# SwiGLU by seven products: 17 inner tiles instead of 14, in another order of products, two of them added onto banks already read; the first two tiles split from float32 copies

## The chip, the cores and the metric

The kernel runs on one core of one Trainium2 chip. The metric is the device time of one execution in microseconds. Three runs of the kernel before took 1377.49, 1380.51 and 1381.48 us, median 1380.51.

## The reference

One decoder layer on 528 columns that matter (16 meta tokens and 512 positions) and 1024 channels: a half-weighted SwiGLU, a mixer (forgetting attention and retention), and a second half-weighted SwiGLU. The change touches the two SwiGLUs alone:

```python
def rmsnorm(x, g):
    y = xf * lax.rsqrt(jnp.mean(xf * xf, axis=-1, keepdims=True) + EPS)
    return y * g

def swiglu(x, w_in, w_out):                       # w_in 1024 x 5632, w_out 2816 x 1024
    a, b = jnp.split(x @ w_in, 2, axis=-1)
    return (jax.nn.silu(a) * b) @ w_out

h = h + 0.5 * swiglu(rmsnorm(h, norm_ffn1), w_ffn1_in, w_ffn1_out)
h = h + mixed(h)                                  # attention, retention, gates, w_out
h = h + 0.5 * swiglu(rmsnorm(h, norm_ffn2), w_ffn2_in, w_ffn2_out)
return h[:, LEAD:]
```

## The kernel before

All activations lie transposed, 128 channels on the partitions and the positions in the free dimension: `h[0..7]`, 128 x 528. Each product in float32 is made of three float32r passes: a tensor is split into a high part and a low part (`split`, lines 104 to 106: ScalarE copies the high part, VectorE subtracts it), and TensorE adds high x high, high x low and low x high (`mm3`, `mm3s`, line 300).

A feed-forward (`ffn`) has 22 inner tiles of 128 channels. Inner tile j has 128 columns of the gate half `a` and 128 of the value half `b` of `w_in`, each over 8 chunks of 128 input channels; one such tile of `w_in` is 1 MB. `SEQ` writes out by hand the order of TensorE's work: `n0 n1` are the first two tiles, `aJ bJ` a plain tile in two halves (48 matmuls each in the first feed-forward, 24 in the second), `uK` sums of the normed input, `eJ lJ` a tile by seven products (`early`, `late`), and `pG` one of the 8 out-projections of tile group G. The four groups have 6, 5, 6 and 5 tiles; each `pG` can only come after its group's last tile. The second feed-forward runs the same sequence on 512 columns instead of 528.

A tile by seven products takes the 2 x 2 blocks (input channels in two halves, positions in two halves of 264 or 256 columns, outputs `a` and `b`) and makes them from seven block products instead of eight. Each block product is 12 matmuls of 264 (256) columns. It needs sums of weight blocks (`wsums`, lines 188 to 191, four VectorE operations of 128 x 512) and of input blocks (`usums`), and sums of the products. VectorE makes these last sums as the products come out of the banks: tiles `b[0]` to `b[3]` from a pool `pq` of 4 PSUM banks. In `early` (lines 403 to 417) four products go to the four banks; in `late` (from line 419) the fifth, sixth and seventh go to banks 0, 2 and 3 again.

TensorE's order is the program's order. In the rest, a scheduler places the instructions of ScalarE (ACT), VectorE (DVE), GpSimd (POOL) and SyncE (SP); each engine then runs its own in order, with semaphores between them. Weights go in pieces of up to 128 x 1024 through rings of 7 high tiles (`wh`) and 5 low ones (`wl`). For a seven-product tile SP loads the whole float32 tile (`w`, two buffers), and ACT and DVE split it and its sums. For all other pieces (kind "w") POOL issues a transfer of the high part (line 201), ACT copies its negative to `wl` (line 227), and POOL issues a second, accumulating transfer onto `wl` (line 228). `weights()` looks ahead: 6 pieces begun, 4 made ready.

At the start SP loads tile 0 of `w_in` in four parts (`w0a`, `w0b`) between the eight `h`; ACT and DVE split it and scale `h` (`gained`, lines 306 and 307). Tile 1 (`n1`) is of kind "w".

Of the kernel before, what the change touches and what calls it, by code (L numbers as in the profile page):

```python
# [25 lines left out]
S = 512  # L26
# [10 lines left out]
          e6 p0 p0 l6 p0 e7 p0 p0 l7 p0 p0 p0  # L37
          e8 l8 e9 a10 l9 b10 e11 p1 l11 p1 p1 e12 p1 l12 p1 e13 p1 l13 p1 p1
          e14 a15 l14 b15 e16 l16 e17 p2 p2 l17 p2 e18 p2 p2 l18 p2 p2 p2
          e19 l19 e20 a21 l20 b21 p3 p3 p3 p3 p3 p3 p3 p3""".split()  # L40
# [24 lines left out]
def layer(tc, order, hT, wf1i, wf1o, wf2i, wf2o, wmix, wsq, vecs, cs, rmask, rvec, cmask, outT):  # L65
# [3 lines left out]
    with ExitStack() as es:  # L69
# [65 lines left out]
        def feed_ffn(seq, w_in, w_out):  # L135
            at_, nxt = {}, [0] * len(PJ)
            for tok in seq:
# [12 lines left out]
                if c in "nae":  # L150
# [3 lines left out]
                        "e": [("A0", "S1"), ("A2", "S0")], "l": [("A1", "S2"), ("A3",)]}[c]  # L154
                pieces.extend((at_[j], x, 1024) for x in cuts)
# [12 lines left out]
        def load(n):  # L168
            while at["l"] < min(n, len(loads)):
                i = at["l"]  # L170
                src, w, kind = loads[i]
                at["l"] += 1
                if kind == "w":
                    raw[i] = src
                    continue
                if st["sp"] is None:
                    at["l"] -= 1
                    return
                raw[i] = st["sp"].tile([128, 2048], F32, name=f"w{i}", tag="wS", bufs=2)
                nc.sync.dma_start(raw[i], src)  # L180
# [12 lines left out]
        def begin(n):  # L193

            while at["c"] < min(n, len(pieces)):
# [4 lines left out]
                if i >= 2 and loads[li][2] == "w":  # L200
                    nc.gpsimd.dma_start(high[i][:, :w], loads[li][0][:, c:c + w])  # L201

        def ready(n):
            begin(n)
            while at["p"] < min(n, len(pieces)):
# [11 lines left out]
                if i < 2:  # L217
                    for x in (0, 512):
                        split(wh[:, x:x + 512], wl[:, x:x + 512], raw[li][i][:, x:x + 512])
                        gained(2 * i + x // 512, gn1, u, 0, "n1")  # L220
                elif loads[li][2] == "S":
                    for x, src in enumerate(c):
                        src = (raw, sums)[src[0] == "S"][li][:, 512 * int(src[1]):512 * int(src[1]) + 512]
                        split(wh[:, 512 * x:512 * x + 512], wl[:, 512 * x:512 * x + 512], src)
# [18 lines left out]
        w0 = [wp.tile([128, 1024], F32, name=f"w0{x}", tag="wl", bufs=5) for x in "ab"]  # L243
        raw[0] = w0
        at["l"] = 1
        for k in range(KC):
            if k < 4:
                nc.sync.dma_start(w0[k // 2][:, 512 * (k % 2):512 * (k % 2) + 512], wf1i[0][:, 512 * k:512 * k + 512])
# [26 lines left out]
        nc.gpsimd.tensor_scalar_mul(kg, kg0, -0.5)  # L275
        R = cp.tile([128, T], F32, name="R")
# [21 lines left out]
        def mm3s(out, w, x, start=True, stop=True):  # L298
            for i, (p, q) in enumerate(((w[0], x[0]), (w[0], x[1]), (w[1], x[0]))):
                nc.tensor.matmul(out, p, q, start=start and i == 0, stop=stop and i == 2)  # L300
# [61 lines left out]
        def ffn(seq, u, gain, a, pst, pq, norm, done, name):  # L362
# [5 lines left out]
            def prod(out, w, off, x, k0, ts, first, last):  # L368

                for k in range(4):  # L370
                    c = slice(off + 128 * k, off + 128 * k + 128)
                    mm3s(out, [z[:, c] for z in w], [z[k0 + k][:, ts] for z in x], first and k == 0, last and k == 3)
# [27 lines left out]
            def early(j):  # L400

                b = [pq(f"{name}q{j}_{x}")[:, :nh] for x in range(4)]
                cu = ttile(f"{name}cu{j}")[:, :2 * nh]
                d = ttile(f"{name}d{j}")[:, :nh]
                bv = ttile(f"{name}b{j}")[:, :2 * nh]
# [12 lines left out]

            def late(j, b, cu, d, bv):
                w = weights()  # L420
                prod(b[0], w, 0, u, 4, t1, True, True)
                prod(b[2], w, 512, u, 4, t2, True, True)
                prod(b[3], weights(), 0, xb, 0, x2, True, True)
                sv = ttile(f"{name}s{j}")[:, :2 * nh]
                nc.vector.tensor_tensor(sv[:, x1], b[0], R[:, t1], ALU.mult)
                nc.vector.tensor_tensor(sv[:, x2], b[2], R[:, t2], ALU.mult)
                nc.vector.tensor_tensor(bv[:, x1], bv[:, x1], b[3], ALU.add)
                nc.vector.tensor_tensor(sv[:, x1], sv[:, x1], cu[:, x1], ALU.add)
                nc.vector.tensor_tensor(sv[:, x2], sv[:, x2], d, ALU.add)
                nc.scalar.activation(sv, sv, AF.Silu)  # L430
# [51 lines left out]
        with tc.tile_pool(name="psA", bufs=1, space=PSUM, reuse_waits="tile") as pA, \  # L482
                tc.tile_pool(name="s1", bufs=1, reuse_waits="tile") as sp1:
            st["sp"] = sp1
# [28 lines left out]
        st["sp"] = None  # L513
        u = nu
# [720 lines left out]
```

## Time and profile before

| | before |
|---|---|
| median of three runs | 1380.51 us (1377.49 to 1381.48) |
| the profiled execution's own time | 1377.54 us |
| its span, first to last instruction | 1375.8 us |
| FFN1, by the timeline of TensorE | 6.1 to about 385 us |
| mixer | about 386 us to 1021 us |
| FFN2 | about 1021 us to 1373 us |
| TensorE's granted clock over the span | 0.998 of full |

All times of rows are microseconds from the span's start, unless marked ns. PE is TensorE, PEld its weight loads. A matmul's own duration overlaps with the next one's, so a tile's time is read from the start of its first matmul to the start of the next tile's first matmul. A number in brackets at a row's end is the engine's idle time just before, and what released it.

### The profile page before, as it was taken

The page shows a single profiled execution, that of the slowest core. Times are in us where ns is not written, and L with a number is a line of the kernel's source. Part 1 is how long each engine was busy: PE and PEld are TensorE (multiplying, and loading weights), DVE is VectorE, ACT ScalarE, POOL GpSimd, SP SyncE. Part 2 cuts the span into 40 slices and gives each one's busy share as a digit, 9 for nine tenths or more (in the row PEclk, how much of TensorE's full clock was granted, in tenths as well). Part 3 has the DMA queues.
Part 4 walks back from the last instruction along what each step waited for, and adds up shares of the span by engine and source line. Part 5 has one row for each costly group of instructions (what it writes and reads, how often), then busy time and mean ns, then how long its engine had stood idle before and what let it go on. Part 6 is the DMA issues. An engine that isn't in the chain of part 4 may idle for free.

```text
span 1375.8 us, 22630 instructions
## 1 busy us (share of the span) xinstructions
PE 1350.0 (98%) x8871; PEld 1229.2 (89%) x8871; DVE 815.5 (59%) x1765; ACT 658.1 (48%) x1131; POOL 319.4 (23%) x462
## 2 busy tenths in 40 slices
PE   6999999999999999999999999999999999999999
PEld 5999999999989788888889998888888889999897
DVE  4876767756456655566654665523337767677552
ACT  5533334332457777777754443553436333343331
POOL 3111111121432323333221212323421111111121
PEclk9999999999999999999999999999999999999999
DMA  9456555574996767767676667889986565565656
GB/s 308 102 145 135 134 145 150 132 158 94 250 239 157 164 144 170 167 150 174 144 184 143 136 143 152 200 211 237 254 205 123 150 133 142 148 161 151 131 126 149
DMA packets 67274, 224.92 MB, mean 163 GB/s; under 512 B 8016, under 2 KB 8400, under 8 KB 63584
## 3 DMA queue, kind: packets, MB, share of 16 engines
q0 software_dynamic: 55936, 181.59, 60.3%
q1 hardware_dynamic: 11088, 41.84, 8.6%
q8 instruction: 70, 1.15, 0.3%
q14 instruction: 36, 0.29, 0.1%
q10 hardware_dynamic: 144, 0.04, 0.0%
HBM read 215.02 MB, written 8.42 MB: 162 GB/s over the span
## 4 chain that ended last, share of the span: by engine, by line
PE 89%; ACT 4%; issue 3%; DVE 2%; DMA 1%; POOL 1%; POOLq 0%; ACTq 0%
PE fq L300 10%; PE sq L300 10%; PE fpo L290 9%; PE spo L290 9%; PE pg L290 5%; PE prv L290 3%; PE oa L290 3%; PE prg L290 3%; PE spa L290 3%; PE spb L290 3%; PE ow L290 3%; PE ob L290 3%; PE fpa L290 3%; PE fpb L290 3%; PE pq L290 3%
## 5 line engine op out<-in xcount | busy, mean ns | idle before, releaser
L227 ACT ACTIVATE wl<-wh 128x1024 fp32r<-128x1024 f32 (+2 forms) x183 | 175.5, 960 | 160.5 <-PE prg L290 23.2
L105 ACT ACTIVATE wh<-w 128x512 fp32r<-128x512 f32 x112 | 70.6, 630 | 255.9 <-PE fq L300 60.9
L106 DVE TENSOR_TENSOR wl<-w,wh 128x512 fp32r<-128x512 f32 x112 | 76.5, 683 | 14.9 <-issue 14.6
L228 POOL DMA_DIRECT2D wl<-in_wmix x65 | 57.3, 881 | 108.2 <-ACT wl L227 94.5
L201 POOL DMA_DIRECT2D wh<-in_wmix x65 | 36.4, 560 | 183.6 <-PE pv L290 32.5
L290 PE MATMUL fpo<-fgl,wh 128*128 128x272 f32 x352 | 71.4, 284 | 0.0
L290 PE MATMUL fpo<-fgh,wh 128*128 128x272 f32 x352 | 71.3, 284 | 0.0
L290 PE MATMUL fpo<-fgh,wl 128*128 128x272 f32 x352 | 71.2, 284 | 0.0
L290 PE MATMUL spo<-sgl,wh 128*128 128x512 f32 (+1 forms) x181 | 70.1, 387 | 0.0
L290 PE MATMUL spo<-sgh,wl 128*128 128x512 f32 (+1 forms) x181 | 70.1, 387 | 0.0
L290 PE MATMUL spo<-sgh,wh 128*128 128x512 f32 (+1 forms) x181 | 70.1, 387 | 0.0
L106 DVE TENSOR_TENSOR pl<-PT,ph 128x512 fp32r<-128x512 f32 (+4 forms) x80 | 33.8, 433 | 47.8 <-ACT ph L105 47.3
L1130 DVE SCALAR_TENSOR_TENSOR hh<-spo,hh 128x512 f32<-128x512 f32 (+1 forms) x33 | 22.2, 674 | 59.7 <-PE spo L290 59.7
L106 DVE TENSOR_TENSOR wl<-ws,wh 128x512 fp32r<-128x512 f32 x84 | 57.5, 684 | 0.0
L105 ACT ACTIVATE wh<-ws 128x512 fp32r<-128x512 f32 x84 | 51.9, 618 | 7.3 <-DVE ws L189 6.4
L290 PEld LDWEIGHTS fpo<-fgh,wl 128*128 128x128 f32 x352 | 54.0, 188 | 0.0
L290 PEld LDWEIGHTS fpo<-fgl,wh 128*128 128x128 f32 x352 | 53.9, 188 | 0.0
L290 PEld LDWEIGHTS fpo<-fgh,wh 128*128 128x128 f32 x352 | 53.9, 188 | 0.0
L290 PE MATMUL pg<-n2uh,wh 128*128 128x512 f32 x128 | 53.8, 421 | 0.0
L505 DVE SCALAR_TENSOR_TENSOR h<-fpo,h 128x528 f32<-128x528 f32 x32 | 22.6, 706 | 48.5 <-PE fpo L290 48.5
L807 ACT ACTIVATE P<-P,st 128x144 f32<-128x144 f32 (+1 forms) x64 | 36.6, 571 | 29.5 <-DVE st L803 28.1
L290 PE MATMUL pg<-n2uh,wl 128*128 128x512 f32 x128 | 50.6, 395 | 0.0
(951 smaller groups left out, 4610.9 us busy)
## 6 DMA issues: line engine op xcount, KB each, us to landing
wh<-in_wmix POOLq DMA_DIRECT2D x65, 512.0 KB, 4.8
wl<-in_wmix POOLq DMA_DIRECT2D x65, 512.0 KB, 7.0
w<-in_wf1i SPq DMA_DIRECT2D x14, 1024.0 KB, 5.1
w<-in_wf2i SPq DMA_DIRECT2D x14, 1024.0 KB, 5.6
wh<-in_wsq POOLq DMA_DIRECT2D x24, 512.0 KB, 5.4
wl<-in_wsq POOLq DMA_DIRECT2D x24, 512.0 KB, 7.8
wh<-in_wf2i POOLq DMA_DIRECT2D x16, 512.0 KB, 5.5
wl<-in_wf2i POOLq DMA_DIRECT2D x16, 512.0 KB, 6.7
```

The source lines that it names most:

```text
L105: nc.scalar.activation(xh, src, AF.Copy)
L106: nc.vector.tensor_tensor(xl, src, f32(xh), ALU.subtract)
L201: nc.gpsimd.dma_start(high[i][:, :w], loads[li][0][:, c:c + w])
L227: nc.scalar.activation(wl[:, :w], f32(wh[:, :w]), AF.Copy, scale=-1.0)
L228: nc.gpsimd.dma_start(wl[:, :w], raw[li][:, c:c + w], accum_op=ALU.add)
L290: nc.tensor.matmul(out, p[:, o:o + 128], q[:, a:b], start=first and k == 0 and i == 0, stop=last and k == nk - 1 and i == 2)
L300: nc.tensor.matmul(out, p, q, start=start and i == 0, stop=stop and i == 2)
L505: nc.vector.scalar_tensor_tensor(h[m][:, x:y], ps, 0.5, h[m][:, x:y], ALU.mult, ALU.add)
L807: last["exp"] = nc.scalar.activation(P[i][:, :w], P[i][:, :w], AF.Exp, scale=-1.0, bias=st[:, 2:3], accum_out=sm[:, 0:1])
L1130: nc.vector.scalar_tensor_tensor(h[m][:, x:y], ps, 0.5, h[m][:, x:y], ALU.mult, ALU.add)
```

## The change

Three things change.

1. `SEQ`: tiles 10, 15 and 21, plain before, become seven-product tiles, so 17 of 22 in each feed-forward instead of 14. The out-projections stand at other places between `e` and `l`.
2. `early` and `late` make the same seven products in another order. `early` now has five: the first to bank 0, the second to bank 1, the third to bank 2, the fourth *added onto bank 0* (`onto`, no clearing at its start), the fifth to bank 3. `late` has two, both in one bank `b` (`fr`, `sr`): the sixth, and the seventh added onto it. VectorE reads such a bank twice, before and after the second product is added: in `early` bank 0 by lines 416 and 423, in `late` by lines 435 and 437. VectorE's sums are 9 operations per tile instead of 11. The pieces of weights are cut as 1024, 512, 1024 and 1024 columns, each split by one ACT and one DVE instruction, instead of seven pairs of 512.
3. The start: tile 1's weights are loaded by SP as float32 (`load(2)`, right behind the last `h`) and split by ACT and DVE, as tile 0's are. POOL's transfers of the next four pieces' high parts wait for a small copy `there` that reads the last `h`. The pool of the float32 tiles is opened before the start for that.

The diff, cut to its core:

```diff
 SEQ = """n0 n1 a2 u0 b2 u1 a3 u2 b3 u3 a4 b4 e5 l5
-          e6 p0 p0 l6 p0 e7 p0 p0 l7 p0 p0 p0
-          e8 l8 e9 a10 l9 b10 e11 p1 l11 p1 p1 e12 p1 l12 p1 e13 p1 l13 p1 p1
-          e14 a15 l14 b15 e16 l16 e17 p2 p2 l17 p2 e18 p2 p2 l18 p2 p2 p2
-          e19 l19 e20 a21 l20 b21 p3 p3 p3 p3 p3 p3 p3 p3""".split()
+          e6 p0 l6 p0 p0 e7 p0 l7 p0 e8 p0 l8 p0 p0
+          e9 l9 e10 l10 e11 p1 l11 p1 e12 p1 l12 p1 p1 e13 p1 l13 p1 p1
+          e14 l14 e15 l15 e16 l16 e17 p2 l17 p2 p2 e18 p2 l18 p2 e19 p2 l19 p2 p2
+          e20 l20 e21 l21 p3 p3 p3 p3 p3 p3 p3 p3""".split()
...
-                        "e": [("A0", "S1"), ("A2", "S0")], "l": [("A1", "S2"), ("A3",)]}[c]
-                pieces.extend((at_[j], x, 1024) for x in cuts)
+                        "e": ["A0", "S2", "S0"], "l": ["A2"]}[c]
+                pieces.extend((at_[j], x, 512 if x == "S2" else 1024) for x in cuts)
...
-                if kind == "w":
+                if kind == "w" and i > 1:
                     raw[i] = src
                     continue
...
-                if i >= 2 and loads[li][2] == "w":
-                    nc.gpsimd.dma_start(high[i][:, :w], loads[li][0][:, c:c + w])
+                if i >= 4 and loads[li][2] == "w":
+                    with tc.issue_after(hold.ins) if i < 8 else ExitStack():
+                        nc.gpsimd.dma_start(high[i][:, :w], loads[li][0][:, c:c + w])
...
+                elif i < 4:
+                    split(wh, wl, raw[li][:, c:c + w])
                 elif loads[li][2] == "S":
-                    for x, src in enumerate(c):
-                        src = (raw, sums)[src[0] == "S"][li][:, 512 * int(src[1]):512 * int(src[1]) + 512]
-                        split(wh[:, 512 * x:512 * x + 512], wl[:, 512 * x:512 * x + 512], src)
+                    o = 512 * int(c[1])
+                    split(wh[:, :w], wl[:, :w], (raw, sums)[c[0] == "S"][li][:, o:o + w])
...
+        there = cp.tile([128, 1], F32, name="there")
+        hold = nc.gpsimd.tensor_copy(there, h[KC - 1][:, 0:1])
...
-            def prod(out, w, off, x, k0, ts, first, last):
+            def prod(out, w, off, x, k0, ts, onto=False):
                 for k in range(4):
                     c = slice(off + 128 * k, off + 128 * k + 128)
-                    mm3s(out, [z[:, c] for z in w], [z[k0 + k][:, ts] for z in x], first and k == 0, last and k == 3)
+                    mm3s(out, [z[:, c] for z in w], [z[k0 + k][:, ts] for z in x], not onto and k == 0, k == 3, onto)
...
             def early(j):
                 b = [pq(f"{name}q{j}_{x}")[:, :nh] for x in range(4)]
...
-                w = weights()
-                prod(b[0], w, 0, u, 0, t1, True, True)
-                nc.vector.tensor_tensor(cu[:, x1], b[0], R[:, t1], ALU.mult)
-                prod(b[1], w, 512, xa, 0, x2, True, True)
-                nc.vector.tensor_tensor(cu[:, x2], cu[:, x1], b[1], ALU.add)
-                w = weights()
-                prod(b[2], w, 512, xa, 0, x1, True, True)
-                nc.vector.tensor_tensor(d, cu[:, x2], b[2], ALU.add)
-                prod(b[3], w, 0, xb, 0, x1, True, True)
-                nc.vector.tensor_tensor(bv[:, x1], cu[:, x2], b[3], ALU.add)
-                nc.vector.tensor_tensor(bv[:, x2], d, b[3], ALU.add)
-                return b, cu, d, bv
+                w = weights()
+                prod(b[0], w, 0, u, 0, t1)
+                nc.vector.tensor_tensor(cu[:, x1], b[0], R[:, t1], ALU.mult)
+                prod(b[1], weights(), 0, u, 4, t2)
+                nc.vector.tensor_tensor(sv[:, x2], b[1], R[:, t2], ALU.mult)
+                v = weights()
+                prod(b[2], v, 512, xa, 0, x2)
+                nc.vector.tensor_tensor(cu[:, x2], cu[:, x1], b[2], ALU.add)
+                prod(b[0], w, 512, u, 4, t1, True)
+                nc.vector.tensor_tensor(sv[:, x1], b[0], R[:, t1], ALU.mult)
+                prod(b[3], v, 0, xa, 0, x1)
+                nc.vector.tensor_tensor(d, cu[:, x2], b[3], ALU.add)
+                nc.vector.tensor_tensor(sv[:, x2], sv[:, x2], d, ALU.add)
+                nc.scalar.activation(sv, sv, AF.Silu)
+                return cu, d, sv
 
-            def late(j, b, cu, d, bv):
-                w = weights()
-                prod(b[0], w, 0, u, 4, t1, True, True)
-                prod(b[2], w, 512, u, 4, t2, True, True)
-                prod(b[3], weights(), 0, xb, 0, x2, True, True)
-                sv = ttile(f"{name}s{j}")[:, :2 * nh]
-                nc.vector.tensor_tensor(sv[:, x1], b[0], R[:, t1], ALU.mult)
-                nc.vector.tensor_tensor(sv[:, x2], b[2], R[:, t2], ALU.mult)
-                nc.vector.tensor_tensor(bv[:, x1], bv[:, x1], b[3], ALU.add)
-                nc.vector.tensor_tensor(sv[:, x1], sv[:, x1], cu[:, x1], ALU.add)
-                nc.vector.tensor_tensor(sv[:, x2], sv[:, x2], d, ALU.add)
-                nc.scalar.activation(sv, sv, AF.Silu)
+            def late(j, cu, d, sv):
+                b = pq(f"{name}r{j}")[:, :nh]
+                bv = ttile(f"{name}b{j}")[:, :2 * nh]
+                w = weights()
+                prod(b, w, 0, xb, 0, x1)
+                nc.vector.tensor_tensor(bv[:, x2], d, b, ALU.add)
+                prod(b, w, 512, xb, 0, x2, True)
+                nc.vector.tensor_tensor(bv[:, x1], cu[:, x2], b, ALU.add)
                 nc.vector.tensor_tensor(sv, sv, bv, ALU.mult)
                 return sv
```

How the order on the engines moves, at three places. TensorE, first feed-forward, inside `late`, where the sixth product ends and the seventh begins; `fq` are the banks of `early`, `fr` the new bank of `late`, `fxbh`/`fxbl` the split input sums. Before (tile 5):

```order
L300 MATMUL fq_2_900<-n1uh_172,wh_691 128x264
L300 MATMUL fq_2_900<-n1ul_173,wh_691 128x264
L300 MATMUL fq_2_900<-n1uh_172,wl_836 128x264
L300 MATMUL fq_3_901<-fxbh_533,wh_780 128x264 [waits DVE_49]
L300 MATMUL fq_3_901<-fxbl_534,wh_780 128x264
L300 MATMUL fq_3_901<-fxbh_533,wl_906 128x264
```

After (tile 6):

```order
L306 MATMUL fr_1154<-fxbh_774,wh_987 128x264
L306 MATMUL fr_1154<-fxbl_775,wh_987 128x264
L306 MATMUL fr_1154<-fxbh_774,wl_1049 128x264
L306 MATMUL fr_1154<-fxbh_534,wh_987 128x264 [waits DVE_49]
L306 MATMUL fr_1154<-fxbl_535,wh_987 128x264
L306 MATMUL fr_1154<-fxbh_534,wl_1049 128x264
```

Before, the seventh product went to bank 3, last filled by the fourth product. Now it goes onto the bank that the sixth has just filled, and its first matmul waits for VectorE.

VectorE, first feed-forward, tile 5, from the sum `d` to the end of the tile's sums; `ws` are weight sums of a coming tile, `wl` splits of its weights, `fs` becomes silu's input, `fb` the value half. Before:

```order
L413 TENSOR_TENSOR fd_903<-fcu_902,fq_2_900 128x264 [waits DVE_49,PE_49]
L415 TENSOR_TENSOR fb_904<-fcu_902,fq_3_901 128x264 [waits PE_49]
L416 TENSOR_TENSOR fb_904<-fd_903,fq_3_901 128x264 [waits DVE_49]
L425 TENSOR_TENSOR fs_1021<-fq_0_898,R 128x264 [waits PE_49]
L428 TENSOR_TENSOR fs_1021<-fs_1021,fcu_902 128x264 [waits DVE_49]
L426 TENSOR_TENSOR fs_1021<-fq_2_900,R 128x264 [waits PE_49]
L429 TENSOR_TENSOR fs_1021<-fs_1021,fd_903 128x264 [waits DVE_49]
L427 TENSOR_TENSOR fb_904<-fb_904,fq_3_901 128x264 [waits PE_49]
L106 TENSOR_TENSOR wl_1072<-w_692,wh_1005 128x512 [waits Activation_49]
L431 TENSOR_TENSOR fs_1021<-fs_1021,fb_904 128x528 [waits DVE_49,Activation_49]
```

After:

```order
L425 TENSOR_TENSOR fd_898<-fcu_897,fq_3_896 128x264 [waits DVE_49,PE_49]
L188 TENSOR_TENSOR ws_1157<-w_1111 128x512 [waits DMAHW1_49,DVE_49]
L426 TENSOR_TENSOR fs_899<-fs_899,fd_898 128x264 [waits DVE_49]
L189 TENSOR_TENSOR ws_1157<-ws_1157,w_1111 128x512 [waits DVE_49]
L435 TENSOR_TENSOR fb_986<-fd_898,fr_985 128x264 [waits PE_49]
L190 TENSOR_TENSOR w_1111<-w_1111 128x512
L191 TENSOR_TENSOR ws_1157<-w_1111,ws_1157 128x512 [waits DVE_49]
L437 TENSOR_TENSOR fb_986<-fcu_897,fr_985 128x264 [waits PE_49]
L438 TENSOR_TENSOR fs_899<-fs_899,fb_986 128x528 [waits DVE_49,Activation_49]
```

The read of `fr` at line 435, for which TensorE's seventh product waits, stands behind two operations on weight sums of 512 columns each.

POOL at the start, from its last constant; `in_wf1i` is `w_in` of the first feed-forward. Before:

```order
L269 CAST bones<-bo_109 128x128 [waits Pool_49]
L201 DMA wh_184<-in_wf1i 128x1024
L201 DMA wh_207<-in_wf1i 128x1024
L201 DMA wh_209<-in_wf1i 128x1024
L201 DMA wh_211<-in_wf1i 128x1024
L201 DMA wh_216<-in_wf1i 128x1024
L228 DMA wl_186<-in_wf1i 128x1024 [waits Activation_49]
```

After:

```order
L273 CAST bones<-bo_113 128x128 [waits Pool_49]
L281 COPY there<-h_84 128x1 [waits DMAHW4_49]
L202 DMA wh_210<-in_wf1i 128x1024
L202 DMA wh_212<-in_wf1i 128x1024
L202 DMA wh_217<-in_wf1i 128x1024
L202 DMA wh_326<-in_wf1i 128x1024 [waits DVE_49,PE_49]
L230 DMA wl_219<-in_wf1i 128x1024 [waits Activation_49]
```

Before, the first accumulating transfer (`wl_186`) was for tile 1. Now it is for tile 2 (`wl_219`); it stands behind a load (`wh_326`) that waits for VectorE and TensorE, and all loads stand behind the copy `there` of the last `h`.

## Rows read from the trace of the kernel before

**Rows 1.** The page: busy time (share of the span) and instructions by engine.

```profile
PE 1350.0 (98%) x8871; PEld 1229.2 (89%) x8871; DVE 815.5 (59%) x1765; ACT 658.1 (48%) x1131; POOL 319.4 (23%) x462
```

**Rows 2.** Waits of TensorE: line, what for, total us, times, longest.

```profile
PE fpa L290 <- DMA wl<-in_wf1i: 6.9, 1, 6.9
...
PE k2pm L648 <- ACT k2sh L105: 2.1, 1, 2.1
```

**Rows 3.** Windows: us, each engine's busy us, granted clock, DMA share, GB/s.

```profile
26.00:32.00 6.00, 3.43 (x15) 3.43 (x16) 0.99 (x2) 1.38 (x2) 2.32 (x3) 0.50 1.08 247
...
100.00:150.00 50.00, 50.00 (x413) 50.00 (x413) 30.05 (x56) 16.21 (x27) 7.16 (x10) 1.00 0.55 135
450.00:500.00 50.00, 46.76 (x276) 39.51 (x275) 29.68 (x98) 36.76 (x78) 16.19 (x23) 1.00 0.76 168
```

**Rows 4.** Timeline of TensorE, tiles 1 and 2: start, us, line, operation.

```profile
21.02 0.41 PE L290 MATMUL fpa<-n1uh,wh 128*128 128x272 f32 x2
...
28.57 0.81 PE L290 MATMUL fpa<-n1uh,wl 128*128 128x272 f32 x2 [6.90 <-DMA wl<-in_wf1i]
...
35.77 0.60 PE L322 MATMUL fpa<-acc,onesD 128*128 128x256 f32 x2
...
42.69 0.29 PE L290 MATMUL fpa<-n1uh,wh 128*128 128x272 f32 x1
...
48.53 0.29 PE L290 MATMUL fpb<-n1uh,wh 128*128 128x272 f32 x1
```

**Rows 5.** Timeline of TensorE: first matmuls of plain and seven-product tiles, FFN1 and FFN2.

```profile
77.73 0.28 PE L300 MATMUL fq<-n1uh,wh 128*128 128x264 f32 x1
...
87.92 0.28 PE L300 MATMUL fq<-n1uh,wh 128*128 128x264 f32 x1
...
1044.13 0.40 PE L290 MATMUL spa<-n3uh,wh 128*128 128x512 f32 x1
...
1055.24 0.40 PE L290 MATMUL spa<-n3uh,wh 128*128 128x512 f32 x1
...
1077.45 0.28 PE L300 MATMUL sq<-n3uh,wh 128*128 128x256 f32 x1
...
1087.40 0.28 PE L300 MATMUL sq<-n3uh,wh 128*128 128x256 f32 x1
```

**Rows 6.** Timelines of TensorE and VectorE: from one to the other, three places.

```profile
105.32 0.29 PE L300 MATMUL fq<-n1uh,wl 128*128 128x264 f32 x1
...
105.64 0.43 DVE L426 TENSOR_TENSOR fs<-fq,R 128x264 f32<-128x264 f32 x1 [0.21 <-PE fq L300]
...
411.44 0.70 DVE L106 TENSOR_TENSOR k0sl<-k0sq,k0sh 128x528 fp32r<-128x528 f32 x1
...
412.19 0.39 PE L649 MATMUL k0pm<-k0sl,bones 128*128 128x272 f32 x1 [1.00 <-DVE k0sl L106]
...
550.12 0.70 DVE L688 TENSOR_TENSOR vr<-pv,R 128x528 f32<-128x528 f32 x1
...
550.97 0.63 PE L692 MATMUL pvt<-ident,vr 128*128 128x128 f32 x4 [0.57 <-DVE vr L688]
```

**Rows 7.** VectorE's groups, 60 to 370 us: count, busy us, mean ns, idle before.

```profile
L415 DVE TENSOR_TENSOR fb<-fcu,fq 128x264 f32<-128x264 f32 x14 | 6.0, 426 | 8.4 <-PE fq L300 8.4
```

**Rows 8.** Timeline of VectorE where nothing makes it wait.

```profile
111.47 0.71 DVE L505 SCALAR_TENSOR_TENSOR h<-fpo,h 128x528 f32<-128x528 f32 x1 [1.70 <-PE fpo L290]
112.10 0.68 DVE L106 TENSOR_TENSOR wl<-w,wh 128x512 fp32r<-128x512 f32 x1
...
113.30 0.42 DVE L408 TENSOR_TENSOR fcu<-fq,R 128x264 f32<-128x264 f32 x1
113.64 0.68 DVE L188 TENSOR_TENSOR ws<-w 128x512 f32<-128x512 f32 x1
```

**Rows 9.** ScalarE's timeline at tile 0's end; the accumulating transfers, 18 to 60 us.

```profile
24.40 0.59 ACT L445 ACTIVATE fsa<-fpa 128x528 f32<-128x528 f32 x1
...
DMA to landing us min/median/max: 6.2/8.4/13.2
```

More of the change, by code (lines that the diff above doesn't have):

```diff
@@ L218, in ready @@
                     for x in (0, 512):
-                        split(wh[:, x:x + 512], wl[:, x:x + 512], raw[li][i][:, x:x + 512])
+                        split(wh[:, x:x + 512], wl[:, x:x + 512], raw[li][:, c + x:c + x + 512])
                         gained(2 * i + x // 512, gn1, u, 0, "n1")
+                elif i < 4:
+                    split(wh, wl, raw[li][:, c:c + w])
                 elif loads[li][2] == "S":
-                    for x, src in enumerate(c):
-                        src = (raw, sums)[src[0] == "S"][li][:, 512 * int(src[1]):512 * int(src[1]) + 512]
-                        split(wh[:, 512 * x:512 * x + 512], wl[:, 512 * x:512 * x + 512], src)
+                    o = 512 * int(c[1])
+                    split(wh[:, :w], wl[:, :w], (raw, sums)[c[0] == "S"][li][:, o:o + w])
                 else:
@@ L242, in layer @@
         h = [atile(f"h{k}") for k in range(KC)]
-        w0 = [wp.tile([128, 1024], F32, name=f"w0{x}", tag="wl", bufs=5) for x in "ab"]
+        s1 = es.enter_context(ExitStack())
+        st["sp"] = s1.enter_context(tc.tile_pool(name="s1", bufs=1, reuse_waits="tile"))
+        w0 = st["sp"].tile([128, 2048], F32, name="w0", tag="wS", bufs=2)
         raw[0] = w0
@@ L247, in layer @@
             if k < 4:
-                nc.sync.dma_start(w0[k // 2][:, 512 * (k % 2):512 * (k % 2) + 512], wf1i[0][:, 512 * k:512 * k + 512])
+                nc.sync.dma_start(w0[:, 512 * k:512 * k + 512], wf1i[0][:, 512 * k:512 * k + 512])
             nc.sync.dma_start(h[k], hT[:, k, :])
@@ L296, in views, with mm3s @@
             return [(ps[:, o + a:o + b], a, b) for a, b in ranges]
-        def mm3s(out, w, x, start=True, stop=True):
+        def mm3s(out, w, x, start=True, stop=True, onto=False):
             for i, (p, q) in enumerate(((w[0], x[0]), (w[0], x[1]), (w[1], x[0]))):
-                nc.tensor.matmul(out, p, q, start=start and i == 0, stop=stop and i == 2)
+                nc.tensor.matmul(out, p, q, start=start and i == 0, stop=stop and i == 2, skip_group_check=onto)
         def gained(k, g, u, a, name):
@@ L404, in early @@
                 d = ttile(f"{name}d{j}")[:, :nh]
+                sv = ttile(f"{name}s{j}")[:, :2 * nh]
+                w = weights()
[6 more added lines that the diff above has]
+                nc.vector.tensor_tensor(cu[:, x2], cu[:, x1], b[2], ALU.add)
@@ L481, in layer @@
         nu = [], []
-        with tc.tile_pool(name="psA", bufs=1, space=PSUM, reuse_waits="tile") as pA, \
-                tc.tile_pool(name="s1", bufs=1, reuse_waits="tile") as sp1:
-            st["sp"] = sp1
+        with tc.tile_pool(name="psA", bufs=1, space=PSUM, reuse_waits="tile") as pA:
             def psA(name):
@@ L513, in layer @@
         st["sp"] = None
+        s1.close()
         u = nu
```

## The prediction

> **What bounds the kernel now.** I read four views, in this order: the page, TensorE's waits, the table of windows, and the timelines of TensorE and VectorE where the change cuts in. The page says that PE is busy 1350 of 1375.8 us [rows 1], so only what PE executes, or what makes it stand still, moves the end. In the first feed-forward (FFN1) the window 100 to 150 us has PE at 50.00 of 50 at full clock; VectorE (DVE) is at 30.05 there, ScalarE (ACT) at 16.21 [rows 3]. So PE waits for nobody between the tiles of a feed-forward today. Its one long wait is 6.90 us, at 28.57, for the low half of inner tile 1's weights [rows 4]; the next longest is 2.1 us, in the mixer [rows 2].
>
> **Part 1, three more tiles by seven products in each feed-forward: a gain.** A plain half tile in FFN1 is 48 matmuls from 42.69 to 48.53, 5.84 us [rows 4], so a plain tile is 11.68. A tile by seven products is 84 matmuls, from 77.73 to 87.92, 10.19 us [rows 5]. Three more: 3 x 1.49 = 4.5 us. In FFN2 a plain tile is 1044.13 to 1055.24, 11.11 us, and one by seven products 1077.45 to 1087.40, 9.95 us [rows 5]: 3 x 1.16 = 3.5 us. PE is the bound in both, so all of it counts: **-8.0 us**. The matmuls of a seven-product tile are as many as before (84); only their banks and order differ.
>
> **Part 2, the first two tiles from float32 copies: a gain.** Before, tile 1's low half was an ACT copy and then an accumulating transfer on POOL's queue. Tile 1's first half takes from 21.02 to 35.77, 14.75 us, where such a half takes 5.84 [rows 4]: 8.9 us lost, 6.90 of it the wait and 2.0 the half clock after it (the window 26 to 32 is granted 0.50, that is 1.2 of 2.4 GHz, [rows 3]). In the changed kernel that low half is a VectorE subtraction from a copy that SyncE has queued right behind the activations, while POOL is held until the last of those has landed. So the copy is early, and the wait goes: **-8.9 us**. What is late next is tile 2. POOL's queue now holds tile 2's accumulating transfer behind a load that waits for the end of tile 0's products (about 21 us), and ACT's copy for it stands behind the copy of tile 0's result (which ran at 24.40, [rows 9]). Started between 22 and 25, with a median 8.4 us to landing [rows 9], it is there at 30.5 to 33.5; PE needs it when tile 1 is through, 21.0 + 2 x 5.84 + 1.1 for the norm's sums (42.69 - 5.84 - 35.77, [rows 4]) = 33.8. That fits with little to spare: I count 0 and keep 0 to 4 us (the wait and some half clock) for the range.
>
> **Part 3, the two products added onto banks already read: a loss.** In `early` the added product stands two products behind the one whose sum is read (the second and third lie between, 2 x 1.45 us), so VectorE has time. In `late` it doesn't: the sixth product fills bank `b`, VectorE must read it alone (`bv` of the second half), and the seventh is added onto the same columns as the very next thing in PE's hand-written order. The order rows show it: the seventh's first matmul waits for VectorE, and nothing stands between. Before, the seventh product's wait was for a read of the fourth's, two products earlier, and cost nothing [rows 3]. PE is in order, so all its later work is queued behind this wait. It falls once in each of 17 tiles, in two feed-forwards: 34 times.
>
> The price of one, from rows: VectorE, idle, starts 0.32 us after the last matmul's start (105.32 to 105.64); the read takes 0.43 (the same operation's group of 14 has a mean of 426 ns, [rows 7]); PE starts 0.05 us after VectorE's end (411.44 + 0.70 to 412.19) or 0.15 (550.12 + 0.70 to 550.97), taken as 0.10 [rows 6]. Less the 0.12 us after which a matmul would start anyhow (10.19 / 84): 0.73 us, with ends of 0.68 and 0.78. **34 x 0.73 = 24.8 us.**
>
> To that comes what VectorE, in order too, has ahead of the read. By starts [rows 8] an operation of 528 columns takes 0.63 us, of 512 0.60, of 264 0.34. One of 1024 (the new wide splits) stands in no row: its ends are 0.63 and 1.20 (two of 512), and by the slope from 264 to 512 columns I take 0.60 + 512 x 0.26 / 248 = 1.14. The Trainium skill ("VectorE: DVE Perf Modes", The TRN2 errata) has a formula for a float32 tensor_tensor, (N + 151) / 0.96 ns, by which such a split lasts 1.22 us, an estimate. For 512 columns it gives 0.69, and a row has 0.68 [rows 8], so the trace agrees there; by it each tile with a wide split ahead would be 0.1 us worse at most, 2 us in all. From the fifth product's end to the read the sixth gives 1.45 us. In tiles 5, 10 and 16 VectorE has 0.34 + 0.60 + 0.34 + 0.60 = 1.88 us to do, in 9, 14, 15 and 20 0.34 + 1.14 + 0.34 = 1.82: late by 0.4. Where an out-projection stands between `early` and `late`, VectorE has the residual (0.63) and a split: with a wide one (7, 11, 18) 1.77, late by 0.3; with a narrow one (6, 8, 12, 13, 17, 19) 1.23, in time. So per feed-forward 7 x 0.4 + 3 x 0.3 = 3.7, in both **7.4 us**. The waits are then 32.2 us, 0.95 each. Low end: the bare price, 34 x 0.68 = 23.1. High end: VectorE half a wide split later each time, 32.2 + 34 x 0.57 = 51.6.
>
> **The rest, at nothing.** VectorE does two operations fewer per tile and 1024-wide splits instead of pairs, but has three more tiles to sum and split: per tile 4 x 0.60 of sums, 3 x 1.14 + 0.60 of splits, 8 x 0.34 and 2 x 0.63, about 10.4 us, against PE's 10.19 + 0.95. It hides behind PE's out-projections (32 in each feed-forward) and now in the waits too; in the longest run without one (tiles 14 to 17) it is nearly as long as PE, which is the third rival. The mixer's VectorE, ScalarE and PE instructions stand in the same order as before.
>
> **Sum.** The profiled execution took 1377.54 us (span 1375.8). 1377.5 - 8.0 - 8.9 + 32.2 = 1392.8. The median of the runs shown, 1380.51, lies 3.0 above that execution; a new median may lie anywhere in between, so I put half of it on top: **1394.3 us**, 1.0% above the median of before.
>
> **Rivals.** (1) *The waits are cheap, and the kernel is not slower.* The place is the same, the 34 waits; below (8.0 + 8.9) / 34 = 0.50 us each the gains win. That needs a round trip shorter than the rows' 0.68: VectorE reading sooner behind the last matmul than 0.32 us, or PE gaining back what it stood by closer matmuls. Against it: three separate rows, each with its part [rows 6]. At 0.45 each: 1377.5 - 16.9 + 15.3 = 1376, and with the half spread 1377.5; at 0.3 each 1372.
>
> (2) *The clock falls.* The window 450 to 500 has PE at 46.76 of 50, with waits of up to 2.1 us, and a granted clock of 1.00 [rows 2, 3]; only the 6.90 us wait went with 0.50. Waits of one microsecond in eleven should leave it alone. If it fell after each, at the 2.0 us that the half clock cost above, 34 x 2.0 = 68 us: 1462; after one in four, 1411. The Trainium skill ("TensorE: Matmul & The Clock Gate", A second HAM failure mode: psum-queue depth-cycling) speaks for this rival: it tells of a kernel whose PE stood briefly at each change of bank, often enough for the clock to swing between its two levels. The window in the mixer speaks against it.
>
> (3) *VectorE becomes the bound in the runs without out-projections.* There PE and VectorE wait for each other in turn, and a late split costs on top of the read. The high end, 51.6 us of waits, would be that: 1377.5 - 16.9 + 51.6 + 1.5 = 1413.7. For it: 10.4 against 11.1 us leaves 7%. Against it: VectorE's order starts each tile's splits one tile ahead.
>
> (4) *The start gives less.* If tile 2's low half is late by 2 us, and the clock falls with it, 4 us come back: 1398.
>
> **How the numbers follow.** The forecast has 0.68, the cheap waits 0.10, the clock 0.05, VectorE as bound 0.10, the late start 0.07. The range reaches from the bare price of the waits with all gains, 1377.5 - 16.9 + 23.1 = 1383.7, to just short of the third rival's 1413.7: 1384 to 1412. What a measurement of this kernel can tell from no change is about 0.3%, 4 us on either side of 1380.5: below 1376.4 lie only waits under 0.42 us each, 0.05; between there and 1384.6 the rest of the cheap waits and the lowest edge of the forecast, 0.10; above it 0.85.
>
> **What would show it.** In the new profile: a wait of PE for VectorE's `bv` line at `fr` and `sr`, 17 times each, 0.6 to 1.0 us long, and PE's busy time in an FFN1 window near 46 of 50. A seven-product tile of 11.1 us against 10.19. No wait for `wl` at 28 us, and a granted clock of 1.00 from 12 us on. I am wrong if those waits total under 17 us, if the granted clock drops inside a feed-forward, or if another wait (for `wl` at tile 2, for splits in tiles 14 to 17) is larger than they are.

## The result and the profile after

| | before | after |
| --- | --- | --- |
| median of four runs, us | 1379.0 (1376.5 to 1381.5) | 1398.9 (1397.8 to 1400.1) |
| profiled execution, us | 1377.5 (span 1375.8) | 1397.9 (span 1395.9) |

The changed kernel is slower: its ratio to the kernel before is 1.0144, with a 95% interval of 1.012 to 1.0168. The forecast was 1394.3 us in a range of 1384 to 1412, so the sign and the range hold, and the measured median lies 4.6 us above the forecast.

The page of the kernel after, busy time by engine and the granted clock in 40 slices of the span, answers [rows 1]. TensorE (PE) is busy for the same 1350 us as before, in a span that is 20.1 us longer. So the loss isn't work that PE does, but waiting. That the busy time is the same is a coincidence, though: by my estimate 8.0 us of products and 2.0 of half clock went, 9.0 came because the profile counts a part of each wait as busy (34.9 us by starts, below, against 25.9 of idle time), and 1.7 came from a fall of the clock in the mixer. The granted clock's digit is 9, that is 90% or more, in every slice; a short fall is too small to show there, and the windows further down show one.

```profile
PE 1350.3 (97%) x8943; PEld 1229.0 (88%) x8943; DVE 839.5 (60%) x1711; ACT 664.3 (48%) x1059; POOL 300.5 (22%) x435
...
PEclk9999999999999999999999999999999999999999
```

The waits of PE in the kernel after (line, what for, total us, times, longest) name where it stands. They answer [rows 2]: the 6.9 us for `wl` are gone, and two new entries are at the top. They are the waits of the seventh product for VectorE's (DVE) read at line 435, 17 in each feed-forward.

```profile
PE sr L306 <- DVE sb L435: 13.0, 17, 1.2
PE fr L306 <- DVE fb L435: 12.9, 17, 1.2
PE fpa L296 <- ACT n1uh L312: 6.4, 1, 6.4
...
PE pff L296 <- issue: 2.2, 1, 2.2
PE k2pm L654 <- ACT k2sh L105: 2.1, 1, 2.1
```

The same three stretches as in [rows 3], from the table of windows of the kernel after. The first, at the start, has PE full and the clock at 1.00, where it was 0.50. The second, in FFN1, has 48.67 of 50 busy. I had forecast "near 46", which would be four waits of 0.95 us; but of the tiles with out-projections only two have their wait in this stretch, with 0.81 and 0.52 us of idle time. (The idle time that the profile puts before a matmul is less than what the wait costs, because the matmul ahead of it counts as busy for 0.28 us, while the next one usually starts after 0.12.) The third, in the mixer, has a granted clock of 0.97, where it was 1.00; the last section comes back to it.

```profile
26.00:32.00 6.00, 6.00 (x49) 5.89 (x48) 1.32 (x3) 5.21 (x8) 1.43 (x2) 1.00 0.98 195
100.00:150.00 50.00, 48.67 (x397) 48.25 (x397) 29.39 (x47) 17.43 (x21) 6.02 (x8) 1.00 0.52 121
450.00:500.00 50.00, 46.42 (x265) 39.43 (x265) 29.98 (x101) 36.61 (x78) 16.98 (x22) 0.97 0.71 168
```

One wait, from the timeline of PE, its weight loads (PEld) and DVE in tile 6 of the kernel after (start, length, engine, line, operation, idle before):

```profile
92.18 0.68 DVE L106 TENSOR_TENSOR wl<-ws,wh 128x512 fp32r<-128x512 f32 x1
...
92.69 0.28 PE L306 MATMUL fr<-fxbh,wl 128*128 128x264 f32 x1
93.02 0.43 DVE L435 TENSOR_TENSOR fb<-fd,fr 128x264 f32<-128x264 f32 x1 [0.15 <-PE fr L306]
93.50 0.19 PEld L306 LDWEIGHTS fr<-fxbh,wh 128*128 128x128 f32 x1 [0.73 <-DVE fb L435]
93.50 0.39 PE L306 MATMUL fr<-fxbh,wh 128*128 128x264 f32 x1 [0.52 <-DVE fb L435]
93.61 0.19 PEld L306 LDWEIGHTS fr<-fxbl,wh 128*128 128x128 f32 x1
93.73 0.29 PE L306 MATMUL fr<-fxbl,wh 128*128 128x264 f32 x1
```

It reads from top to bottom. DVE is done with its split at 92.86 and idle. The sixth product's last matmul starts at 92.69, the read 0.33 us later, the seventh product's first matmul 0.48 after that: 0.81 us from start to start, where 0.12 is usual. Then comes one thing that the forecast lacks. Weight load and matmul start together at 93.50, and the next matmul only at 93.73, 0.23 us behind and not 0.12. One row further the load (93.61) is again 0.12 us ahead of its matmul (93.73). That the missing lead is what makes the start late is my reading; no run tried it.

By segments of the profiled executions, each from the start of one matmul to that of another (the first column from the span's start; "middle" is everything from FFN1's last out-projection to FFN2's first seven-product tile, the mixer above all):

| | to first seven-product tile | FFN1 from there to last out-projection | middle | FFN2, same | rest | span |
| --- | --- | --- | --- | --- | --- | --- |
| before | 77.73 | 306.19 | 693.53 | 294.80 | 3.51 | 1375.8 |
| after | 68.23 | 319.73 | 695.15 | 309.20 | 3.59 | 1395.9 |
| own bank | 69.01 | 302.50 | 698.29 | 293.16 | 3.60 | 1366.6 |
| start only | 70.43 | 306.19 | 693.68 | 294.80 | 3.40 | 1368.5 |
| old products | 70.21 | 302.15 | 694.76 | 292.69 | 3.59 | 1363.4 |
| out-projection between | 68.92 | 311.58 | 696.52 | 303.17 | 3.59 | 1383.8 |
| fourteen tiles | 68.36 | 322.14 | 692.65 | 310.58 | 3.42 | 1397.1 |
| second read | 68.88 | 325.64 | 691.99 | 314.85 | 3.58 | 1404.9 |

The last six rows are the experiments below. The kernel after wins 9.5 us at the start and loses 13.5 and 14.4 in the two feed-forwards.

### The profile page after: what moved, and what is told of

Its sections match the earlier page's. It is cut to its first block, busy times and chain, and to the rows that moved or that the text cites. A ratio compares the mean times of both kernels' runs of the same rounds, so it can differ in the third digit from the quotient of the medians.

```text
span 1395.9 us, 22534 instructions
## 1 busy us (share of the span) xinstructions
PE 1350.3 (97%) x8943; PEld 1229.0 (88%) x8943; DVE 839.5 (60%) x1711; ACT 664.3 (48%) x1059; POOL 300.5 (22%) x435
## 4 chain that ended last, share of the span: by engine, by line
PE 82%; DVE 7%; issue 4%; ACT 4%; POOL 1%; DMA 1%; SPq 0%; POOLq 0%; ACTq 0%
PE spo L296 9%; PE sq L306 8%; PE fq L306 8%; PE fpo L296 7%; PE pg L296 5%; PE prv L296 3%; PE oa L296 3%; PE prg L296 3%; PE ob L296 3%; PE ow L296 3%; PE pq L296 3%; PE sr L306 3%; PE fr L306 3%; PE pk L296 3%; PE fpb L296 2%
## 5 line engine op out<-in xcount | busy, mean ns | idle before, releaser
L105 ACT ACTIVATE wh<-w 128x1024 fp32r<-128x1024 f32 (+1 forms) x74 | 76.7, 1037 | 123.8 <-PE fq L306 24.8
L106 DVE TENSOR_TENSOR wl<-w,wh 128x1024 fp32r<-128x1024 f32 (+1 forms) x74 | 88.1, 1190 | 7.8 <-ACT wh L105 7.5
L202 POOL DMA_DIRECT2D wh<-in_wf1o x32 | 17.8, 557 | 209.9 <-DVE wl L106 56.0
L202 POOL DMA_DIRECT2D wh<-in_wf2o x32 | 17.9, 559 | 203.3 <-DVE wl L106 54.0
L306 PE MATMUL fq<-n1uh,wh 128*128 128x264 f32 x204 | 58.1, 285 | 0.0
L306 PE MATMUL fq<-n1ul,wh 128*128 128x264 f32 x204 | 57.9, 284 | 0.0
L306 PE MATMUL fq<-n1uh,wl 128*128 128x264 f32 x204 | 57.9, 284 | 0.0
L306 PE MATMUL sq<-n3uh,wl 128*128 128x256 f32 x204 | 57.5, 282 | 0.0
L306 PE MATMUL sq<-n3uh,wh 128*128 128x256 f32 x204 | 57.4, 281 | 0.0
L306 PE MATMUL sq<-n3ul,wh 128*128 128x256 f32 x204 | 57.3, 281 | 0.0
```

The lines of the kernel that those rows point to most:

```text
L105: nc.scalar.activation(xh, src, AF.Copy)
L106: nc.vector.tensor_tensor(xl, src, f32(xh), ALU.subtract)
```

## Experiments

**The seventh product in its own bank.** If the waits are the loss, a kernel that keeps all of the change but the second accumulation should gain all of it back.

```diff
-                prod(b, w, 512, xb, 0, x2, True)
+                b2 = pq(f"{name}z{j}")[:, :nh]
+                prod(b2, w, 512, xb, 0, x2)
                 nc.vector.tensor_tensor(bv[:, x1], cu[:, x2], b, ALU.add)
+                nc.vector.tensor_tensor(bv[:, x1], bv[:, x1], b2, ALU.add)
```

> The changed kernel, with the seventh product of a tile put into a bank of its own and added by one more VectorE operation; the 17 tiles, the new order of the products, the wide splits and the new start all stay. Theory (the loss is the 34 waits of the seventh product for VectorE's read of the bank just filled, 1.03 us each from start to start in the profile after, 34.9 us in all): no wait of PE at fr and sr is left, the time is 1398.9 - 34.9 = 1364.0 us, which is 0.989 of the kernel before, with 3 us either way. Rival (the loss is VectorE's load in the new order: wide splits, three more tiles to sum and split): the waits come back at other tiles and with one operation more per half tile; 1385 to 1399 us. Rival (the start or the clock costs something): the time stays above 1370 without any wait at these tiles.

Measured: 1368.1 us, 0.9918 of the kernel before (0.9903 to 0.9933). All 34 waits are gone. The top of PE's waits in this kernel:

```profile
PE fpa L296 <- ACT n1uh L312: 6.2, 1, 6.2
PE pff L296 <- issue: 4.4, 1, 4.4
PE pvt L700 <- DVE vr L696: 2.8, 5, 0.6
```

The new bank is one of the same pool of four. In the table FFN1 is 17.2 us shorter than in the kernel after, FFN2 16.0. Counting only the seven-product tiles (the sum of the intervals from one matmul's start to the next) it is 17.2 and 17.1, together 34.3 us, 1.01 for each wait. One more DVE operation in each tile costs nothing that shows there; the 1.1 us between 16.0 and 17.1 lie at the end of FFN2, where two matmuls of an out-projection now wait for ACT and DVE (idle for 0.3 and 0.2 us). So the waits are the loss to within a microsecond or two, and neither the new order of products nor DVE's load is. The time is 4 us above what I expected, for a reason elsewhere: 3.1 us lie in the middle segment, where PE stood 4.4 us at the change to the mixer and the clock fell (below). In two of its five runs the granted clock was 1.000 and 0.999 over the span, not 0.996 to 0.998 as in the others, and these two took 1364.8 and 1364.5 us.

**The new start alone.** The kernel before with the changed pieces, loads, splits and hold of the first two tiles; the order of the tiles and the products are those of before. Its edit is the start's part of the change.

> The kernel before, with the new start alone (the first two tiles' copies and splits); 14 tiles by seven products in the old order and with the old banks. Theory: the wait of 6.9 us for tile 1's weights goes and the half clock behind it; the tile that follows the five plain ones starts 9.5 us earlier, as in the profile after; 1379.0 - 9.5 = 1369.5 us, 0.993 of the kernel before. Rival (what is gained at the start is given back at tile 2 or later by transfers that are now later): 1374 to 1379 us with a wait for wl in tiles 2 to 5.

Measured: 1368.5 us, 0.9929 (0.9913 to 0.9945). This is the forecast's second part by itself: 7.3 us in the table and 9.5 by the medians (the kernel before, run beside it, took 1378.0), with FFN1 and FFN2 to 0.01 us as before. No wait for `wl` of tile 2 follows. The 2.2 us between this run and the kernel after at the first mark lie in PE's first matmuls: in this run PE stands 0.96 us until 9.08 for ACT's split of tile 0, and its matmuls come at full rate later. The window from 12 to 16 us of this kernel, and the same of the kernel after:

```profile
12.00:16.00 4.00, 4.00 (x25) 4.00 (x25) 3.62 (x6) 3.85 (x7) 1.98 (x4) 1.00 1.04 429
```

```profile
12.00:16.00 4.00, 4.00 (x35) 4.00 (x34) 3.56 (x6) 3.84 (x6) 1.99 (x4) 1.00 1.02 420
```

PE is full in both, with 25 matmuls in the one and 35 in the other. Six matmuls take 1.32 us until 14.5 us in this run, and 0.73 from 10.9 us on in the kernel after. The 1.00 of these rows says nothing of that: the trace's list of granted clocks has its first entry at 14.69 us in this run and at 10.42 in the kernel after, and a window counts time ahead of the first entry as 1.00. In all eight kernels the matmuls double their rate within about 0.3 us of that entry; ahead of it they come at 0.22 us, as they do at the lower level of 1.2 GHz (15 in 3.43 us, [rows 3]).

**Seventeen tiles and the start, with the old products.** The order of tiles and the start of the changed kernel, with `early`, `late` and the splits of before; nothing is added onto a bank that was read.

> The changed kernel with its 17 tiles and its start, but with the seven products in the order, the banks and the splits of before, so that nothing is added onto a bank that was read. Theory: 8.0 us of gain from three more such tiles in each feed-forward and 9.5 from the start, no waits: 1379.0 - 17.5 = 1361.5 us, 0.987 of the kernel before. Rival (three more tiles make VectorE the bound in the runs of tiles without an out-projection between them, whatever the banks): waits for wl or for banks of 0.5 us and more in tiles 9 to 16, 1368 us or more.

Measured: 1365.8 us, 0.9915 (0.9902 to 0.9929). It is the fastest kernel of the study by its median, 12 us below the kernel before as run beside it and 33 below the kernel after; its interval covers the two above. Against the start alone, the three more tiles save 4.04 us in FFN1 and 2.11 in FFN2, 6.2 of the 8.0 that I counted. A part of what is missing stands in this kernel's waits between 60 and 370 us, and between 1065 and 1362:

```profile
PE fq L307 <- DVE fd L420: 0.2, 1, 0.2
```

```profile
PE sq L307 <- DVE sd L420: 0.4, 1, 0.4
PE spo L297 <- DVE sgl L106: 0.2, 1, 0.2
```

Counted by starts, with the late second matmul behind each, they come to 1.5 us. The third rival is there in its beginnings, then, far from the 3 us that I had named for it: DVE is late at three places, each time by half a microsecond from start to start at most. The start gave 7.5 us here, 2.0 less than I had put in; PE came to full rate at about 14.5 us, as in the run above.

**An out-projection between the sixth and the seventh product.** The same products, banks and splits; `late` is cut in two, and in nine tiles of 17 an out-projection that stood next to the tile goes between.

```diff
-          e6 p0 l6 p0 p0 e7 p0 l7 p0 e8 p0 l8 p0 p0
+          e6 p0 l6 p0 k6 p0 e7 p0 l7 p0 k7 e8 p0 l8 p0 k8 p0
...
                 prod(b, w, 0, xb, 0, x1)
                 nc.vector.tensor_tensor(bv[:, x2], d, b, ALU.add)
+                return b, bv, w, cu, sv
+
+            def last(j, b, bv, w, cu, sv):
                 prod(b, w, 512, xb, 0, x2, True)
```

> The changed kernel with the same products, banks and splits; only in 9 of the 17 tiles of a feed-forward (6, 7, 8, 11, 12, 13, 17, 18, 19) one out-projection that stood elsewhere beside the tile is put between the sixth and the seventh product. Theory (what costs is that the seventh product comes directly behind the one whose bank VectorE must read): 18 of the 34 waits are gone, 16 stay with 1.18 us each, 18.9 us of 34.9; 1398.9 - 16.0 = 1382.9 us, 1.003 of the kernel before. Rival (the price lies in adding onto a bank that was read, or in VectorE's load, wherever the product stands): 34 waits or the same idle time elsewhere, 1395 to 1400 us.

Measured: 1385.0 us, 1.0052 (1.0039 to 1.0066). PE's waits in this kernel:

```profile
PE sr L306 <- DVE sb L435: 7.5, 8, 1.2
PE fr L306 <- DVE fb L435: 7.3, 8, 1.2
```

The 18 waits are gone and 16 stand, as expected. All 34 seventh products are still added onto a bank that was read; only the nine tiles of each feed-forward where PE has other work in between pay nothing. What costs is the order, not the accumulation. The feed-forwards are 14.2 us shorter than in the kernel after, of 16.0 expected; two new waits in out-projections of FFN2, for the transfer of their weights' low half (0.9 and 0.6 us idle, together 1.8 us more than usual from start to start), take the rest.

**Fourteen tiles.** The changed kernel with the order of tiles of before (the `SEQ` of before, nothing else).

> The changed kernel with the 14 seven-product tiles of before in place of 17 (the order of tiles of before); the new products, banks, splits and start stay. Theory (each such tile has its price in the wait): 28 waits and not 34; against the changed kernel 8.0 us of gain are lost and 6 x 1.03 = 6.2 us of waits saved, 1.8 us more: 1400.7 us, 1.016 of the kernel before. Rival (three more tiles are what loads VectorE so much): 5 us and more below the changed kernel, 1394 us or less.

Measured: 1398.6 us, 1.0134 (1.0114 to 1.0155), with 28 waits. The whole time is that of the changed kernel, but by chance. In the table the feed-forwards are 2.4 and 1.4 us longer than after, where 1.8 in all was expected, because the 28 waits are dearer in the mean than the 34 (1.12 against 1.04 us from start to start); so the three tiles give 3.8 us more than the waits that come with them take. The middle segment is 2.5 us shorter here and hides this in the whole. The rival, in which the three tiles load DVE, needed 5 us less; it is out.

**A second read.** One more DVE operation, directly behind the first read and of its shape, from the same bank.

```diff
                 nc.vector.tensor_tensor(bv[:, x2], d, b, ALU.add)
+                nc.vector.tensor_tensor(bv[:, x1], cu[:, x2], b, ALU.add)
                 prod(b, w, 512, xb, 0, x2, True)
```

> The changed kernel, with a second VectorE read of the same bank, of the same shape, directly behind the first and before the seventh product; what it writes is written over later. Theory (PE stands for VectorE's read, and what VectorE has ahead is in line with it): each of the 34 waits grows by one operation of 264 or 256 columns, 0.34 us from start to start in a row of VectorE behind each other, 0.43 at most: 34 x 0.34 = 11.6 to 34 x 0.43 = 14.6 us; 1410.5 to 1413.5 us, 1.023 to 1.025 of the kernel before. Rival (PE does not stand for the read, but for the bank or for its own restart): within 4 us of the changed kernel.

Measured: 1408.4 us, 1.0211 (1.019 to 1.0232), 9.6 above the changed kernel. In the two feed-forwards it is 5.9 and 5.7 us, 0.34 for each wait, the lower end of what I expected; the middle segment of this profiled run is 3.2 us shorter and hides a part in the whole. The same place as above, in tile 6 of this kernel:

```profile
94.01 0.43 DVE L435 TENSOR_TENSOR fb<-fd,fr 128x264 f32<-128x264 f32 x1 [0.16 <-PE fr L306]
94.35 0.42 DVE L436 TENSOR_TENSOR fb<-fcu,fr 128x264 f32<-128x264 f32 x1
94.83 0.19 PEld L306 LDWEIGHTS fr<-fxbh,wh 128*128 128x128 f32 x1 [1.07 <-DVE fb L436]
94.83 0.39 PE L306 MATMUL fr<-fxbh,wh 128*128 128x264 f32 x1 [0.86 <-DVE fb L436]
```

The idle time went from 0.52 to 0.86, by just the 0.34 us that one more operation in a row takes. The time from the last read's end to PE's start is 0.05 us in the mean in both, and the late second matmul behind it is the same too.

## Why the prediction was right, point by point

**What bounds the kernel.** Right: what PE executes and what makes it stand still account for the time, to within the 1.4 us named below. But the profile's split into busy and idle time isn't that account: busy time moved by 0.3 us, the net of four larger terms (above).

**Part 1, three more tiles: -8.0 us.** Right in what the tiles give: between the fourteen tiles and the kernel after, the feed-forwards differ by 3.8 us and the waits by 4.0, together 7.8. Against the kernel before less arrives: 27.9 us of loss in the feed-forwards are 34.9 us of waits (below) less 8.0, and 1.0 that I can't assign. With the old products the same three tiles gave 6.2, and 1.5 of the missing 1.8 are the small waits shown.

**Part 2, the start: -8.9 us.** Right: -9.5 in the changed kernel and -7.3 by itself, and they differ by how soon PE's first matmuls came at full rate. The first entries of the clock's list are at 12.00 us in the kernel before, 10.42 in the changed one and 14.69 in the start alone. Half of each difference taken off, the gain is about 8.7 us in both, an estimate; what the changed kernel has above that is luck, which no term of the forecast foresaw. Tile 2's low half was in time in every run, so the fourth rival is out.

**Part 3, the waits: +32.2 us.** The mechanism, the place and the number are right; the size is 34.9 us, 1.03 for each and not 0.95. From the sixth product's last matmul to the seventh's first it is 1.04 us in the mean, 0.92 more than usual, 31.4 in all: my sum was 32.2. Two errors nearly cancel in it: PE starts 0.05 us behind VectorE's end in every wait and not 0.10, about 1.6 us less in all, and the late reads cost about 8.2 us and not 7.4. In `early`, as forecast, the added product costs nothing: neither `fq` nor `sq` is among PE's waits. The classes hold as well, but for tile 20. Four rows of PE's timeline in the kernel after, of tiles 5, 9, 20 and 21:

```profile
78.13 0.39 PE L306 MATMUL fr<-fxbh,wh 128*128 128x264 f32 x1 [0.97 <-DVE fb L435]
...
157.91 0.39 PE L306 MATMUL fr<-fxbh,wh 128*128 128x264 f32 x1 [0.90 <-DVE fb L435]
...
346.31 0.39 PE L306 MATMUL fr<-fxbh,wh 128*128 128x264 f32 x1 [1.22 <-DVE fb L435]
...
357.31 0.39 PE L306 MATMUL fr<-fxbh,wh 128*128 128x264 f32 x1 [0.52 <-DVE fb L435]
```

From the start of the matmul ahead they are 1.25, 1.18, 1.50 and 0.80 us. The forecast, with the 0.12 of a usual start added, was 1.25 for the first three (0.73 + 0.40 + 0.12) and 0.85 for the last. What VectorE has ahead of the read in tile 9 of the kernel after, from its timeline:

```profile
155.61 0.42 DVE L425 TENSOR_TENSOR fd<-fcu,fq 128x264 f32<-128x264 f32 x1
155.95 1.22 DVE L106 TENSOR_TENSOR wl<-w,wh 128x1024 fp32r<-128x1024 f32 x1
157.09 0.43 DVE L426 TENSOR_TENSOR fs<-fs,fd 128x264 f32<-128x264 f32 x1
157.43 0.42 DVE L435 TENSOR_TENSOR fb<-fd,fr 128x264 f32<-128x264 f32 x1
```

By starts that is 0.34 + 1.14 + 0.34, the forecast's own sum, and the 1.14 that I took for a wide split by a slope is what it takes. (It lasts 1.22 us and the next operation starts before its end. The Trainium skill's formula, "VectorE: DVE Perf Modes", The TRN2 errata, gives the 1.22, and the trace agrees.) In tile 20 the order is another, and so is the sum:

```profile
343.69 0.42 DVE L425 TENSOR_TENSOR fd<-fcu,fq 128x264 f32<-128x264 f32 x1
344.15 0.43 DVE L426 TENSOR_TENSOR fs<-fs,fd 128x264 f32<-128x264 f32 x1
344.69 1.23 DVE L106 TENSOR_TENSOR wl<-w,wh 128x1024 fp32r<-128x1024 f32 x1
345.84 0.42 DVE L435 TENSOR_TENSOR fb<-fd,fr 128x264 f32<-128x264 f32 x1
```

Here `fs` stands directly behind `fd`, which it reads, and starts 0.46 us behind it; the split follows after 0.54. The sum is 2.15 and not 1.82.

The term that I left out is the restart. The first matmul behind a wait lets the next one start after 0.225 us in the mean, against 0.121: 34 x 0.104 = 3.5 us. The trace of before shows it, at the very place from which I took PE's start behind VectorE [rows 6]. Behind the matmul that waited, at 412.19, PE's timeline of the kernel before goes on:

```profile
412.42 0.28 PE L648 MATMUL k0pm<-k0sh,bones 128*128 128x256 f32 x1
412.54 0.28 PE L649 MATMUL k0pm<-k0sl,bones 128*128 128x256 f32 x1
```

The next one starts 0.23 us behind it, and the one after that 0.12. I had read on to where the waiting matmul starts, and not one row further.

**The sum.** For the profiled execution I had 1392.8 us, and 1397.9 came. The 5.1 us between are +2.7 of waits, -0.6 at the start, +1.6 in the middle segment, +1.0 in the feed-forwards, and 0.4 at the end and around the span. The 1.6 in the middle is no more than that segment varies between kernels in which the mixer is the same: 692.0 to 698.3 in the table; here a fall of the clock stands in it (last section).

**The signs.** The waits stand where I said, 17 and 17, with 0.5 to 1.2 us idle before each and not 0.6 to 1.0. A seven-product tile takes 11.26 us in FFN1 and 11.01 in FFN2 in the mean, where I had 11.1 for FFN1. There is no wait for `wl` at 28 us. Two signs failed without touching the argument: the window near 46 (it has 48.67), and a granted clock of 1.00 from 12 us on, which the mixer broke once.

**The rivals.** Cheap waits: no, 0.80 us from start to start is the shortest class. The clock: it did not fall in the feed-forwards, with 34 stops of PE of 0.5 to 1.2 us, nor in the second read's, with stops of up to 1.6. The kernel that the Trainium skill tells of ("TensorE: Matmul & The Clock Gate", A second HAM failure mode: psum-queue depth-cycling), in which short stops were enough to make the clock swing, has no counterpart here: this trace shows no such swing. VectorE as the bound: no, and even the second read added only itself.

## What to carry to other kernels

Adding a product onto a bank that another engine must read first cost nothing here where PE had two products (in `early`) or an out-projection to do in between, and a full round trip where it was the next thing in PE's order: 0.33 us to the read, 0.43 for it, 0.05 back, and 0.1 for a late second matmul, 0.8 us with the usual start taken off. Price such a wait from the last matmul before it to the second one behind it, then count what the reading engine has ahead of the read. A bank of its own for the last product bought back all 34 us here, and one out-projection moved in between bought back the wait of every tile that had one at hand. About 8 us of the 34.9 are reads that come late behind VectorE's other work; whether another order on VectorE alone gets these back was not tried. And ask what the accumulation is for: with the waits gone, the feed-forwards with the new products are 0.8 us longer than with the old ones (302.50 + 293.16 against 302.15 + 292.69 in the table). VectorE's two operations fewer bought nothing, since it was not the bound.

## What was not expected of the hardware

A fall of the clock goes with the length of the middle segment: the five longest in the table (698.3 to 693.7 us) have a stretch of 5 us in the mixer with a granted clock under 0.8, the three shortest (693.5 to 692.0) have none. In the kernel with the seventh product in its own bank, PE's matmul at 376.21 stood idle for 4.42 us, and the windows around it show the granted clock at its lower level of 1.2 GHz (0.50) from inside that stop on (the first one ends before the stop does, and has 0.90 already):

```profile
370.00:375.00 5.00, 1.78 (x15) 1.58 (x14) 1.54 (x4) 2.21 (x3) 1.26 (x2) 0.90 1.07 296
375.00:380.00 5.00, 3.79 (x17) 3.83 (x18) 1.99 (x4) 2.59 (x4) 1.07 (x2) 0.50 1.10 289
380.00:385.00 5.00, 5.00 (x37) 4.88 (x36) 0.50 (x1) 1.52 (x3) 0.55 (x1) 0.92 1.08 284
```

In the kernel after, the idle time at this change was 2.2 us and the clock stayed. It fell at another place of the mixer, behind the wait of 2.1 us for `k2sh`, which ends at 460.67:

```profile
455.00:460.00 5.00, 3.57 (x29) 3.30 (x28) 2.94 (x16) 4.88 (x15) 1.85 (x3) 1.00 1.01 191
460.00:465.00 5.00, 3.84 (x14) 3.16 (x15) 4.05 (x8) 3.54 (x7) 1.91 (x3) 0.66 0.93 229
```

In the kernel before, the same wait of the same length left the clock at 1.00 [rows 2, 3]. So a stop of 2.1 us stands on either side here. Shorter ones do too: in the own-bank kernel the clock fell again behind a stop of 1.33 us for `k2sh` that ends at 447.62, while in the second read a stop of 1.64 us for the same tile, which ends at 465.83, left it at 1.00. The own-bank kernel's windows:

```profile
445.00:450.00 5.00, 3.18 (x19) 2.50 (x18) 4.18 (x11) 5.00 (x10) 1.69 (x3) 0.91 0.99 241
450.00:455.00 5.00, 5.00 (x22) 4.11 (x21) 2.95 (x5) 3.65 (x7) 0.77 (x2) 0.75 0.82 190
```

The length of a stop alone doesn't tell, then. The stops of 0.5 to 1.2 us, 17 in each feed-forward, all stand on the side where nothing falls. Why the wait at 376 us was 4.4 us in the one kernel and 2.2 in the other was not tried, and stays open. So does what makes the clock rise at 10.4 us in one run and at 14.7 in another.
